# Twelve places for the experts' weights joined to six of 16 KB a partition

## The chip, the cores and the metric

The kernel runs on one core of a Trainium2 chip. What counts is the device time of one execution in microseconds (us); the time before is the median of three runs.

## The reference, cut to what matters

A sequence of 256 tokens of width 1024 goes through one transformer block of another kind (`first_block`) and then through two layers of the same kind. All arithmetic is in float32. A layer of the second part is a mixer (two attentions whose results are gated and merged) and a set of 16 experts, of which each chooses 32 tokens for itself.

```python
def hybrid_mixer(h, w_in, w_branch_a, w_branch_b, b_gate, sink_logit, w_out):
    proj = jnp.einsum('bsd,dc->bsc', h, w_in)
    qa, ka, va, qw, kw, vw, gates = jnp.split(proj, SPLITS, axis=-1)
    ...
    ya = jnp.einsum('bsc,cd->bsd', oa.reshape(B, S, DIL_OUT), w_branch_a)
    ...
    yb = jnp.einsum('bsc,cd->bsd', ob.reshape(B, S, WIN_Q), w_branch_b)
    g = jax.nn.sigmoid((gates + b_gate)...).reshape(B, S, N_BRANCH_2, D)
    merged = g[:, :, 0] * ya + g[:, :, 1] * yb
    return jnp.einsum('bsd,de->bse', merged, w_out)

def expert_choice_ffn(h, w_router, w_gate, w_up, w_down):
    cap = CAPACITY_FACTOR * S // N_EXPERTS          # 32 tokens
    aff = jax.nn.softmax(jnp.einsum('bsd,de->bse', h, w_router)..., axis=-1)
    gate, idx = lax.top_k(jnp.swapaxes(aff, 1, 2), cap)
    xe = h[bidx, idx]
    a = jnp.einsum('becd,edf->becf', xe, w_gate)
    u = jnp.einsum('becd,edf->becf', xe, w_up)
    ye = jnp.einsum('becf,efd->becd', jax.nn.silu(a) * u, w_down)
    return jnp.zeros_like(h).at[bidx, idx].add(gate[..., None] * ye)
```

Each expert has three weights of 1024 x 1024 float32 (4 MB each), so the experts of one layer read 192 MB and multiply each weight with 32 tokens only.

## The kernel before, in words

**Dense products.** Every dense weight comes in loads of one megabyte (`load`, L118: 128 partitions of 2048 floats) into a ring of three tiles named `w`. `split_w` makes of each half of such a tile (`hf` 0 and 1) a rounded high part on ScalarE (L124) and the remaining low part on VectorE (L125), in tiles `ws`; `mm3` (L130 to L132) then multiplies three times: high by high, high by low, low by high. A ring tile is free for its next load when both its halves are split. SP issues all of these loads, in the order of the program, and an issue that has to wait holds up those behind it.

**Mixer.** The loads of `w_in2` are numbered 0 to 22 by their second index. After the attentions, `gate(j)` takes the loads 15 + 2j and 16 + 2j, multiplies, and applies a tanh on ScalarE (L927). Between the gates lie the products of the branches: `w_br2` gives five loads, each tile's halves serve eight blocks of 128 columns (`blk`), and after ten blocks `merge` joins two results: VectorE adds them, ScalarE writes the high part of `M` (L270) and VectorE its low part. The order of the text is the order of the engines' queues: `gate(0)`, `gate(1)`, branch products for i = 0 and 1, `gate(2)`, two more, `gate(3)`, and the rest. So ScalarE's queue holds, in one row, the splits of loads 18 to 20, the cast of the attention's result `Y` (L157), the tanh of the gates and the copies for `M`.

**Experts.** A layer's 192 MB are cut into 192 chunks of one megabyte, 128 rows of 8 KB (`CH` = 2048 floats). `grouped` (L1172) takes them in order with `take()` and runs 16 matmuls on each, with four experts side by side on the array. `Experts.load` issues a chunk (L1045) into the next place of a fixed cycle of 21: `q`, four `a0`, six `a1`, `Ha`, `Hb`, `b`, three ring tiles `r`, four split tiles `s`; the first round has two more, `x`. In the profile the places' tiles are named `we`, and the two of `x` `W` and `XB`. The chunks of a layer's end (its last 16) skip `Ha` and `Hb` and are issued one behind the other, and the last chunk comes in two halves (128 x 1024).

```python
self.cycle = ["q"] + ["a0"] * NA0 + ["a1"] * NA + ["Ha", "Hb"] + ["b"] * NB + ["r"] * RING + ["s"] * NSPLIT
self.places = self.cycle + ["x", "x"]
...
src = a["w_exp"][self.l, i]
...
def pace(self):
    if len(self.have) < 1 + NA0 + NA:
        self.load(True)
```

**Chunks ahead of their layer.** While the mixer runs, the first places are filled: `prefetch(1, True)` in the query part, `pace()` behind each load of the gates and branches, and `prefetch(2, True)` at i = 5. A load that is paced this way first gets a copy of one column on GpSimd (L1040) from the newest split tile, so that it can't start before that split has been made. When the mixer ends, the remaining places are asked for with `take()` and from then on each place as soon as its last reader has ended.

`act_pair()` gives the two tiles `Ha` and `Hb` for the high and low part of the normed input, which the places of the same names reuse while the experts run.

Of the kernel before, what the change touches and what calls it, by code (L numbers as in the profile page):

```python
# [18 lines left out]
P = 128  # L19
# [36 lines left out]
ENDS = ((0, 512), (512, 256), (768, 256))  # L56

SCRATCH = 2048


@with_exitstack
def tile_net(ctx: ExitStack, tc: tile.TileContext, a, out):
# [98 lines left out]
    def act_pair():  # L161
        return tuple(hp.tile([P, KT, T], F32R, name=f"H{c}", tag=f"H{c}") for c in "ab")
# [531 lines left out]
    def mixer(l, h, stats, w0=None):  # L694

        with ExitStack() as es:
# [17 lines left out]
            xl.r2a.append(late.enter_context(tc.tile_pool(name=f"e{l}a0", bufs=NA0, side="right", reuse_waits="tile")))  # L714
# [83 lines left out]
            for i in range(4):  # L798
                parts_q(qws[i], load(w1[l, 2 + i]))
                xl.prefetch(1, True)  # L800
# [57 lines left out]
            xl.prefetch(1, True)  # L858
# [51 lines left out]
            xl.r2a.append(late.enter_context(tc.tile_pool(name=f"e{l}a", bufs=NA, side="right", reuse_waits="tile")))  # L910
# [21 lines left out]
            for i in range(8):  # L932
                if i % 2 == 0 and i < 6:
                    gate(i // 2 + 1)
                if i == 5:

                    xl.prefetch(2, True)
                ps = psd()
                for k in range(10):
                    if blk % 16 == 0:  # L940
                        w = load(a["w_br2"][l, blk // 16])
                        xl.pace()
                    if blk % 8 == 0:
                        wh, wl = split_w(sp, w, blk // 8 % 2)
                    b = blk % 8 * P
                    mm3(ps[:, 0:T] if k < 2 else ps[:, T:], cols(wh, b, P), cols(wl, b, P),
                        Y[:, 0, k, :], Y[:, 1, k, :], k in (0, 2), k in (1, 9))
                    blk += 1
                merge(M, i, [tgs[i // 2][:, b, i % 2, :] for b in range(2)], [ps[:, 0:T], ps[:, T:]])
# [58 lines left out]
    class Experts:  # L1008


        def __init__(self, l):
            self.l, self.r2a, self.r2b, self.at, self.dma = l, [], None, 0, None
            self.have, self.n = [], 0

            self.cycle = ["q"] + ["a0"] * NA0 + ["a1"] * NA + ["Ha", "Hb"] + ["b"] * NB + ["r"] * RING + ["s"] * NSPLIT
            self.places = self.cycle + ["x", "x"]

        def load(self, paced=False):
            i = len(self.have)
            end = i >= NCHUNK - sum(cn for _, cn in ENDS) * KT // 512  # L1020
            while True:
                where = self.places.pop(0)
                if not self.places:
                    self.places = list(self.cycle)

                if not (end and where in ("Ha", "Hb")):
                    break
            if where == "x":
                t = self.extra.pop(0).rearrange("p a d -> p (a d)")
            elif where == "s":  # L1030
                t = sp.tile([P, 2, 1024], F32, name="we", tag="ws").rearrange("p a d -> p (a d)")
            else:
                pool, tag = {
                    "q": (qp, "Qb"), "a0": (self.r2a[0], "w2"), "a1": (self.r2a[-1], "w2"), "b": (self.r2b, "w3"),
                    "r": (ring, "w"), "Ha": (hp, "Ha"), "Hb": (hp, "Hb"),
                }[where]
                t = pool.tile([P, CH], F32, name="we", tag=tag)
# [3 lines left out]
            src = a["w_exp"][self.l, i]  # L1041

            for c0, cn in ((0, 1024), (1024, 1024)) if i == NCHUNK - 1 else ((0, CH),):
                with tc.issue_after(self.dma.ins) if end else nullcontext():
                    self.dma = nc.sync.dma_start(t[:, c0 : c0 + cn], src[:, c0 : c0 + cn])  # L1045
            self.have.append(t)
# [5 lines left out]
        def pace(self):  # L1052

            if len(self.have) < 1 + NA0 + NA:
# [8 lines left out]
    def experts(l, last, xl, bp, xg, lg, rt):  # L1063
        nonlocal x
        with ExitStack() as es:
# [165 lines left out]
            for g in range(4):  # L1231
# [27 lines left out]
                else:  # L1259
                    if not last:  # L1260
                        h = act_pair()
                    for i, (c0, cn) in enumerate(ENDS):
                        if not last and c0 + cn == D:
                            xl.prefetch(NCHUNK - len(xl.have))
# [49 lines left out]
def _experts(*ws):  # L1314
# [11 lines left out]
    return np.concatenate(chunks, 0)  # L1326
# [139 lines left out]
```

## Time and profile before

| what | value |
|---|---|
| median of three runs | 1898.48 us (1895.02 to 1900.64) |
| the profiled execution | 1898.55 us, span 1896.8 us |
| mean granted clock of TensorE in it | 0.888 of full speed |
| TensorE busy | 1600.4 us, 84% of the span |
| VectorE / ScalarE / GpSimd busy | 823.2 / 629.2 / 46.3 us |
| moved by DMA | 562.49 MB, mean 297 GB/s |

The span runs from the first to the last instruction that the profiler recorded on the core; the device time of the same execution is 1.75 us longer. Busy shares are means over stretches of different kinds. In the slices of the page the first block ends near 500 us, the mixers take some 500 to 750 us and 1160 to 1430 us, and between and behind them lie the experts, where the rate of the transfers is highest and VectorE and ScalarE have next to nothing to do.

### The profile page before, as it was taken

The numbers are of one execution on the slowest core, as the hardware profiler recorded it, in microseconds if no ns is written. First come the engines' busy times: TensorE is split into PE (matmuls) and PEld (weight loads), VectorE is DVE, ScalarE is ACT, GpSimd is POOL, SyncE is SP. The second block draws the span as 40 slices with busy tenths as digits, with TensorE's granted clock in tenths as the row PEclk, the third lists the DMA queues.
The fourth block names the chain that finished last, engine by engine and source line by source line (L and its number), as shares of the span: only waits on it lengthen the run. The fifth ranks groups of instructions, "written<-read, shape, count | busy, mean of one in ns | idle before, by whom it ended". The sixth has DMA issues, their size and how long they took to land.

```text
span 1896.8 us, 27588 instructions
## 1 busy us (share of the span) xinstructions
PE 1600.4 (84%) x11434; PEld 1081.8 (57%) x11434; DVE 823.2 (43%) x1481; ACT 629.2 (33%) x1130; POOL 46.3 (2%) x72
## 2 busy tenths in 40 slices
PE   8999999999999988876767666999898866766665
PEld 7899999999998987220111102888896311101101
DVE  7688787996687556100000001687464100000001
ACT  5567646666566443100000001566443100000001
POOL 0100000000011000000000000010000000000000
PEclk9999999999999999887777768999999887867768
DMA  6454554554553367999999999832577999999998
GB/s 248 167 190 167 178 178 179 187 190 178 217 223 112 147 267 275 397 419 420 420 420 419 420 420 418 332 129 102 222 266 277 418 420 419 419 420 419 420 421 321
DMA packets 83829, 562.49 MB, mean 297 GB/s; under 512 B 9452, under 2 KB 14456, under 8 KB 16888
## 3 DMA queue, kind: packets, MB, share of 16 engines
q1 hardware_dynamic: 83544, 560.20, 74.7%
q8 instruction: 90, 1.47, 0.3%
q10 hardware_dynamic: 160, 0.52, 0.1%
q14 instruction: 35, 0.29, 0.0%
HBM read 558.84 MB, written 1.85 MB: 296 GB/s over the span
## 4 chain that ended last, share of the span: by engine, by line
PE 54%; DMA 43%; DVE 2%; ACT 1%; issue 0%; SPq 0%; ACTq 0%; DVEq 0%
DMA we<-in_w_exp_dram 42%; PE ps_d L130 14%; PE ps_d L131 14%; PE ps_d L132 14%; PE ps_t L257 1%; PE ps_g L1172 1%; PE ps_v L846 1%; DMA w<-in_w_in_dram 1%; PE ps_u L1172 1%; PE ps_s L772 1%; PE ps_s L878 1%; PE ps_s L773 0%; PE ps_s L374 0%; PE ps_t L1187 0%; PE ps_v L896 0%
## 5 line engine op out<-in xcount | busy, mean ns | idle before, releaser
L130 PE MATMUL ps_d<-Ha,ws 128*128 128x256 f32 x1408 | 404.9, 288 | 14.7 <-ACT Ha L177 7.9
L132 PE MATMUL ps_d<-Ha,ws 128*128 128x256 f32 x1408 | 404.9, 288 | 5.0 <-DVE ws L125 4.9
L131 PE MATMUL ps_d<-Hb,ws 128*128 128x256 f32 x1408 | 403.6, 287 | 0.7 <-DVE Hb L178 0.7
L125 DVE TENSOR_TENSOR ws<-w,ws 128x1024 fp32r<-128x1024 f32 x282 | 342.6, 1221 | 119.7 <-ACT ws L124 117.0
L124 ACT CAST ws<-w 128x1024 fp32r<-128x1024 f32 x282 | 293.3, 1047 | 256.0 <-PE ps_d L132 223.3
L130 PEld LDWEIGHTS ps_d<-Ha,ws 128*128 128x128 f32 x1408 | 273.0, 194 | 18.4 <-ACT Ha L177 7.9
L132 PEld LDWEIGHTS ps_d<-Ha,ws 128*128 128x128 f32 x1408 | 273.0, 194 | 8.3 <-DVE ws L125 6.1
L131 PEld LDWEIGHTS ps_d<-Hb,ws 128*128 128x128 f32 x1408 | 272.9, 194 | 3.5 <-issue 1.2
L1172 PE MATMUL ps_u<-we,W 128*32 128x512 f32 x992 | 187.8, 836 | 90.4 <-DMA we<-in_w_exp_dram 90.3
L1172 PE MATMUL ps_g<-we,W 128*32 128x512 f32 x1024 | 175.9, 789 | 71.9 <-DMA we<-in_w_exp_dram 71.8
L1172 PE MATMUL ps_e<-we,W 128*32 128x512 f32 (+1 forms) x1152 | 162.6, 669 | 64.2 <-DMA we<-in_w_exp_dram 64.1
L1172 PEld LDWEIGHTS ps_u<-we,W 128*32 128x32 f32 x992 | 25.4, 125 | 239.2 <-DMA we<-in_w_exp_dram 223.1
L1172 PEld LDWEIGHTS ps_g<-we,W 128*32 128x32 f32 x1024 | 26.5, 123 | 205.7 <-DMA we<-in_w_exp_dram 165.3
L1246 ACT ACTIVATE W<-ps_g 128x512 f32<-128x512 f32 x16 | 9.6, 597 | 381.4 <-PE ps_g L1172 381.4
L1172 PEld LDWEIGHTS ps_e<-we,W 128*32 128x32 f32 x1152 | 29.4, 120 | 163.6 <-DMA we<-in_w_exp_dram 121.1
L1248 DVE SCALAR_TENSOR_TENSOR W<-W,ps_u 128x512 f32<-128x512 f32 x16 | 11.0, 688 | 247.1 <-PE ps_u L1172 247.1
L1201 DVE COPY W<-ps_e 128x512 f32<-128x512 f32 (+1 forms) x18 | 11.4, 632 | 221.5 <-PE ps_e L1172 221.5
L1247 DVE SCALAR_TENSOR_TENSOR W<-W,ps_g 128x512 f32<-128x512 f32 x16 | 11.0, 688 | 208.1 <-ACT W L1246 208.1
L1253 ACT COPY W<-ps_t 128x512 f32<-128x512 f32 x16 | 9.4, 586 | 275.9 <-PE ps_t L1252 275.9
L130 PE MATMUL ps_d<-Y,ws 128*128 128x256 f32 x288 | 81.4, 283 | 0.0
L132 PE MATMUL ps_d<-Y,ws 128*128 128x256 f32 x288 | 81.4, 283 | 0.0
L131 PE MATMUL ps_d<-Y,ws 128*128 128x256 f32 x288 | 81.4, 282 | 0.0
(327 smaller groups left out, 2371.9 us busy)
## 6 DMA issues: line engine op xcount, KB each, us to landing
we<-in_w_exp_dram SPq DMA_DIRECT2D x378, 1024.0 KB, 19.9
w<-in_w_in_dram SPq DMA_DIRECT2D x46, 1024.0 KB, 4.9
w<-in_w_up_dram SPq DMA_DIRECT2D x22, 1024.0 KB, 4.8
w<-in_w_br_dram SPq DMA_DIRECT2D x18, 1024.0 KB, 4.9
w<-in_w_gate_dram SPq DMA_DIRECT2D x12, 1024.0 KB, 4.9
w<-in_w_out_dram SPq DMA_DIRECT2D x12, 1024.0 KB, 4.9
w<-in_w_down_dram SPq DMA_DIRECT2D x11, 1024.0 KB, 4.9
w<-in_w_rnn_dram SPq DMA_DIRECT2D x8, 1024.0 KB, 4.8
```

The costliest lines, as they stand in the source:

```text
L124: nc.scalar.copy(ws[:, 0], s)
L125: nc.vector.tensor_tensor(ws[:, 1], s, ws[:, 0].bitcast(F32), op=ALU.subtract)
L130: nc.tensor.matmul(ps, wh, xh, start=first, stop=False)
L131: nc.tensor.matmul(ps, wh, xl, start=False, stop=False)
L132: nc.tensor.matmul(ps, wl, xh, start=False, stop=last)
L257: nc.tensor.transpose(ps[:, i * P : i * P + P], b, ident)
L772: nc.tensor.matmul(ps, q, kh, start=True, stop=False)
L846: nc.tensor.matmul(po[64 * c : 64 * c + 64, :T], vw[:, k, kvh * 64 : kvh * 64 + 64], pts[c][:, k * T : k * T + T], start=k == 0, stop=k == 1,)
L878: nc.tensor.matmul(ps[:, o], qa[b, i, tk], ka[b, i, kr], start=True, stop=True)
L1172: nc.tensor.matmul(b[32 * e : 32 * e + 32, :cn], lhs[:, k, 32 * e : 32 * e + 32], cols(w, ((k - k0) * 4 + e) * cn, cn), start=k == 0, stop ...
L1201: nc.vector.tensor_copy(ye[:, s], E[:, :cn])
L1247: nc.vector.scalar_tensor_tensor(th, th, 1.0, G[n], op0=ALU.add, op1=ALU.mult)
```

## The change

Three kinds of places are joined in pairs: the four `a0` become two, the six `a1` three, and `Ha` and `Hb` one place `H`, each now 16 KB in every partition. A joined place is filled by one load of two megabytes, in 128 rows of 16 KB, and holds two chunks that follow each other; the host lays these two out as such rows. A list made ahead (`_plan`) says for each load its first chunk, the number of chunks and its place, and the host and the kernel both follow it. All other places keep one chunk of 128 rows of 8 KB, as do the last four chunks of a layer; a joined `H` that would reach into the last 16 is skipped. The cycle of places and the total room in SBUF stay the same. The chunks ahead of their layer are asked for in fewer and larger pieces: `prefetch` is called at three places of the query part's loop and not at two others, `pace()` does something on every second call only, and `prefetch(2, True)` becomes `prefetch(1, True)`. The two tiles of `act_pair()` are now halves of one.

```diff
+def _plan():
+    cycle = [("q", 1)] + [("a0", 2)] * (NA0 // 2) + [("a1", 2)] * (NA // 2) + [("H", 2)] + [("b", 1)] * NB
+    cycle += [("r", 1)] * RING + [("s", 1)] * NSPLIT
+    places, plan, i = cycle + [("x", 1)] * 2, [], 0
+    while i < NCHUNK:
+        where, n = places.pop(0)
+        places = places or list(cycle)
+
+        if where == "H" and i + n > NCHUNK - LAST:
+            continue
+        n = n if i < NCHUNK - 4 else 1
+        plan.append((i, n, where))
+        i += n
+    return plan
...
     def act_pair():
-        return tuple(hp.tile([P, KT, T], F32R, name=f"H{c}", tag=f"H{c}") for c in "ab")
+        H = hp.tile([P, 2, KT, T], F32R, name="H", tag="H")
+        return H[:, 0], H[:, 1]
...
             for i in range(4):
                 parts_q(qws[i], load(w1[l, 2 + i]))
-                xl.prefetch(1, True)
+                if i != 2:
+                    xl.prefetch(1, True)
...
             parts_q(qa0, load(w1[l, 6]))
-            xl.prefetch(1, True)
...
                 if i == 5:
 
-                    xl.prefetch(2, True)
+                    xl.prefetch(1, True)
...
         def load(self, paced=False):
...
+            i, m, where = self.plan.pop(0)
+            end = i >= NCHUNK - LAST
...
-                t = pool.tile([P, CH], F32, name="we", tag=tag)
+                size = 2 * CH if where in ("a0", "a1", "H") else CH
+                t = pool.tile([P, size], F32, name="we", tag=tag)
...
-            src = a["w_exp"][self.l, i]
...
+            src = a["w_exp"][self.l, i * P * CH : (i + m) * P * CH].rearrange("(p c) -> p c", p=P)
...
-            self.have.append(t)
+            self.have += [t[:, CH * j : CH * j + CH] for j in range(m)]
...
-            if len(self.have) < 1 + NA0 + NA:
+            self.asked += 1
+            if self.asked % 2 and len(self.have) < 1 + NA0 + NA:
                 self.load(True)
...
-    return np.concatenate(chunks, 0)
+    chunks = np.concatenate(chunks, 0)
+    return np.concatenate([chunks[i : i + n].transpose(1, 0, 2).reshape(-1) for i, n, _ in _plan()])
```

**SP's queue in the gates.** The first row is the first branch load of the first layer (`w_br2` 0), the second the next one; `w_7839` is load 19 of `w_in2`, `w_7899` load 20. Before:

```order
L118 DMA w_7743<-in_w_br2_dram 128x2048
L118 DMA w_7810<-in_w_br2_dram 128x2048
L1045 DMA we_7546<-in_w_exp_dram 128x2048
L1045 DMA we_7609<-in_w_exp_dram 128x2048
L1045 DMA we_7673<-in_w_exp_dram 128x2048
L118 DMA w_7839<-in_w_in2_dram 128x2048
L1045 DMA we_7736<-in_w_exp_dram 128x2048
L1045 DMA we_7745<-in_w_exp_dram 128x2048
L118 DMA w_7899<-in_w_in2_dram 128x2048
L1045 DMA we_7812<-in_w_exp_dram 128x2048
L118 DMA w_8006<-in_w_br2_dram 128x2048
```

and with the change, where `w_7821` is load 19 and `w_7881` load 20:

```order
L137 DMA w_7728<-in_w_br2_dram 128x2048
L137 DMA w_7795<-in_w_br2_dram 128x2048
L137 DMA w_7821<-in_w_in2_dram 128x2048
L1056 DMA we_7537<-in_w_exp_dram 128x4096
L1056 DMA we_7661<-in_w_exp_dram 128x4096
L1056 DMA we_7730<-in_w_exp_dram 128x4096
L137 DMA w_7881<-in_w_in2_dram 128x2048
L137 DMA w_7988<-in_w_br2_dram 128x2048
```

Load 19 stands right behind the second branch load now, and three joined loads of the experts stand between it and load 20, where three single ones stood ahead of load 19 and two between.

**ScalarE's queue at the same place.** L124 are the splits' high parts; `w_7680` is load 18, `w_7743` and `w_7810` the branch loads, `w_7839` load 19. Before:

```order
L124 CAST ws_7682<-w_7680 128x1024
L258 COPY pd_7423<-ps_t_7462 128x512
L157 CAST Y_5875<-ps_v_7468 128x256
L124 CAST ws_7709<-w_7680 128x1024
L124 CAST ws_7748<-w_7743 128x1024
L124 CAST ws_7775<-w_7743 128x1024
L927 ACTIVATE tg_7615<-tg_7615,hb_5873 128x256 x2
L124 CAST ws_7815<-w_7810 128x1024
L927 ACTIVATE tg_7615<-tg_7615,hb_5873 128x256 x2
L270 ACTIVATE M_7487<-m0_7784 128x256
L124 CAST ws_7841<-w_7839 128x1024
L124 CAST ws_7868<-w_7839 128x1024
```

With the change L143 are the splits; `w_7668` is load 18, `w_7728` and `w_7795` the branch loads, `w_7821` load 19. The rows begin with the second half of load 18:

```order
L143 CAST ws_7697<-w_7668 128x1024
L278 COPY pd_7414<-ps_t_7453 128x512
L176 CAST Y_5872<-ps_v_7459 128x256
L143 CAST ws_7733<-w_7728 128x1024
L143 CAST ws_7760<-w_7728 128x1024
L947 ACTIVATE tg_7603<-tg_7603,hb_5870 128x256 x2
L143 CAST ws_7797<-w_7795 128x1024
L143 CAST ws_7823<-w_7821 128x1024
L947 ACTIVATE tg_7603<-tg_7603,hb_5870 128x256 x2
L143 CAST ws_7850<-w_7821 128x1024
L290 ACTIVATE M_7478<-m0_7769 128x256
```

The second half of load 18 has moved ahead of the cast of `Y` (L157 before, L176 now); the first half of load 19 has moved to right behind the branch half, and both its halves stand ahead of the copies for `M` (L270 before, L290 now).

**SP's queue in the first layer's experts.** The names `W` and `XB` are the two places `x` at the end of the first round. Before:

```order
L1045 DMA W<-in_w_exp_dram 128x2048
L1045 DMA XB<-in_w_exp_dram 128x2048
L1045 DMA we<-in_w_exp_dram 128x2048 x168
L1045 DMA we<-in_w_exp_dram 128x1024 x2
L719 DMA sinks<-in_rows_dram 128x32
```

and with the change, where 128x4096 is a joined load:

```order
L1056 DMA W<-in_w_exp_dram 128x2048
L1056 DMA XB<-in_w_exp_dram 128x2048
L1056 DMA we<-in_w_exp_dram 128x2048 x2
L1056 DMA we<-in_w_exp_dram 128x4096
L1056 DMA we<-in_w_exp_dram 128x2048 x2
L1056 DMA we<-in_w_exp_dram 128x4096 x2
L1056 DMA we<-in_w_exp_dram 128x2048 x2
L1056 DMA we<-in_w_exp_dram 128x4096 x3
L1056 DMA we<-in_w_exp_dram 128x2048 x4
L1056 DMA we<-in_w_exp_dram 128x4096 x6
L1056 DMA we<-in_w_exp_dram 128x2048 x9
L1056 DMA we<-in_w_exp_dram 128x4096 x6
```

The row of single loads behind `XB` has become an alternation of joined and single ones; its later rounds are six joined and nine single loads each, and the layer ends with ten single loads and the two halves.

## Rows read from the trace of the kernel before

**Rows 1.** The page's span and its queues: packets, MB, share of 16 engines.

```profile
span 1896.8 us, 27588 instructions
...
q1 hardware_dynamic: 83544, 560.20, 74.7%
q8 instruction: 90, 1.47, 0.3%
```

**Rows 2.** Stretches: length, busy PE PEld DVE ACT POOL, PEclk, DMA share, GB/s.

```profile
650.00:745.00 95.00, 90.14 (x722) 86.44 (x722) 56.04 (x89) 40.90 (x59) 3.98 (x7) 0.98 0.73 279
783.00:1144.00 361.00, 253.35 (x1386) 54.47 (x1378) 24.69 (x39) 14.30 (x31) 0.00 (x0) 0.74 1.01 420
1466.00:1868.00 402.00, 279.26 (x1575) 58.86 (x1571) 27.62 (x44) 16.34 (x35) 0.00 (x0) 0.77 1.01 420
```

**Rows 3.** The chain that ended last, by line, in shares of the span.

```profile
DMA we<-in_w_exp_dram 42%; PE ps_d L130 14%; PE ps_d L131 14%; PE ps_d L132 14%; PE ps_t L257 1%; PE ps_g L1172 1%; PE ps_v L846 1%; DMA w<-in_w_in_dram 1%; PE ps_u L1172 1%; PE ps_s L772 1%; PE ps_s L878 1%; PE ps_s L773 0%; PE ps_s L374 0%; PE ps_t L1187 0%; PE ps_v L896 0%
```

**Rows 4.** DMA issues (KB, us to landing); SP's waits (us, times, longest).

```profile
we<-in_w_exp_dram SPq DMA_DIRECT2D x378, 1024.0 KB, 19.9
...
SPq L1045 <- DMA we<-in_w_exp_dram: 667.1, 316, 3.6
```

**Rows 5.** The chain in the second expert stretch: start us, us, what.

```profile
1483.54 19.90 DMA we<-in_w_exp_dram
...
1503.50 18.66 DMA we<-in_w_exp_dram
...
1522.23 19.89 DMA we<-in_w_exp_dram
```

**Rows 6.** The load queue from 147.5 to 149.5 us: packets, MB, share.

```profile
q1 hardware_dynamic: 143, 0.13, 20.9%
```

**Rows 7.** The load queue from 510 to 512 us.

```profile
q1 hardware_dynamic: 118, 0.88, 104.6%
```

**Rows 8.** ScalarE's timeline, 643 to 648.2 us: start, us, instruction, idle before.

```profile
646.44 1.05 ACT L124 CAST ws<-w 128x1024 fp32r<-128x1024 f32 x1 [0.91 <-PE ps_d L132]
```

**Rows 9.** ScalarE's timeline from 652 to 680 us.

```profile
652.62 0.37 ACT L157 CAST Y<-ps_v 128x256 fp32r<-128x256 f32 x1 [4.64 <-PE ps_v L902]
652.89 2.95 ACT L124 CAST ws<-w 128x1024 fp32r<-128x1024 f32 x3
...
664.42 0.42 ACT L270 ACTIVATE M<-m 128x256 fp32r<-128x256 f32 x1 [2.91 <-DVE m L269]
664.75 1.98 ACT L124 CAST ws<-w 128x1024 fp32r<-128x1024 f32 x2
...
675.64 0.91 ACT L927 ACTIVATE tg<-tg,hb 128x256 f32<-128x256 f32 x2 [7.27 <-DVE tg L213]
676.45 2.93 ACT L124 CAST ws<-w 128x1024 fp32r<-128x1024 f32 x3
```

**Rows 10.** SP's timeline from 640 to 662 us.

```profile
642.78 0.33 SPq L118 DMA_DIRECT2D w<-in_w_br_dram  x1
643.16 11.00 SPq L1045 DMA_DIRECT2D we<-in_w_exp_dram  x3
655.74 0.33 SPq L118 DMA_DIRECT2D w<-in_w_in_dram  x1
...
658.48 0.39 SPq L118 DMA_DIRECT2D w<-in_w_in_dram  x1
```

**Rows 11.** TensorE's waits, 650 to 745 us: us, times, longest.

```profile
PE ps_d L130 <- ACT ws L124: 2.7, 1, 2.7
PE ps_d L132 <- DVE ws L125: 2.2, 1, 2.2
```

**Rows 12.** Stretches behind the waits, columns as in rows 2.

```profile
679.00:683.00 4.00, 4.00 (x23) 4.00 (x23) 3.14 (x3) 1.43 (x2) 0.00 (x0) 0.57 0.53 150
1366.00:1369.00 3.00, 3.00 (x17) 3.00 (x17) 0.59 (x2) 0.00 (x0) 0.00 (x0) 0.58 0.99 396
1375.00:1379.00 4.00, 3.94 (x20) 3.94 (x21) 3.50 (x3) 2.66 (x4) 0.00 (x0) 0.57 0.17 23
```

**Rows 13.** The chain where the experts begin: start us, us, what.

```profile
763.91 1.85 PE ps_g L1172 x16
```

More of the change, by code (lines that the diff above doesn't have):

```diff
@@ L56 @@
 ENDS = ((0, 512), (512, 256), (768, 256))
+LAST = sum(cn for _, cn in ENDS) * KT // 512
 SCRATCH = 2048
+def _plan():
[11 more added lines that the diff above has]
+    return plan
 @with_exitstack
@@ L713, in mixer @@
             xl = Experts(l)
-            xl.r2a.append(late.enter_context(tc.tile_pool(name=f"e{l}a0", bufs=NA0, side="right", reuse_waits="tile")))
+            xl.r2a.append(late.enter_context(tc.tile_pool(name=f"e{l}a0", bufs=NA0 // 2, side="right", reuse_waits="tile")))
             att = es.enter_context(ExitStack())
@@ L909, in mixer @@
             att.close()
-            xl.r2a.append(late.enter_context(tc.tile_pool(name=f"e{l}a", bufs=NA, side="right", reuse_waits="tile")))
+            xl.r2a.append(late.enter_context(tc.tile_pool(name=f"e{l}a", bufs=NA // 2, side="right", reuse_waits="tile")))
             M = qp.tile([P, 2, KT, T], F32R, name="M", tag="Qa")
@@ L1012, in __init__ @@
             self.l, self.r2a, self.r2b, self.at, self.dma = l, [], None, 0, None
-            self.have, self.n = [], 0
-            self.cycle = ["q"] + ["a0"] * NA0 + ["a1"] * NA + ["Ha", "Hb"] + ["b"] * NB + ["r"] * RING + ["s"] * NSPLIT
-            self.places = self.cycle + ["x", "x"]
+            self.have, self.n, self.plan, self.asked = [], 0, _plan(), 0
         def load(self, paced=False):
[L1019 to L1027, printed above, removed]
+            i, m, where = self.plan.pop(0)
+            end = i >= NCHUNK - LAST
             if where == "x":
@@ L1034, in load @@
                     "q": (qp, "Qb"), "a0": (self.r2a[0], "w2"), "a1": (self.r2a[-1], "w2"), "b": (self.r2b, "w3"),
-                    "r": (ring, "w"), "Ha": (hp, "Ha"), "Hb": (hp, "Hb"),
+                    "r": (ring, "w"), "H": (hp, "H"),
                 }[where]
-                t = pool.tile([P, CH], F32, name="we", tag=tag)
+                size = 2 * CH if where in ("a0", "a1", "H") else CH
+                t = pool.tile([P, size], F32, name="we", tag=tag)
             if paced:
                 nc.gpsimd.tensor_copy(t[:, 0:1], turn[0][:, 0:1].bitcast(F32))
-            src = a["w_exp"][self.l, i]
-            for c0, cn in ((0, 1024), (1024, 1024)) if i == NCHUNK - 1 else ((0, CH),):
+            src = a["w_exp"][self.l, i * P * CH : (i + m) * P * CH].rearrange("(p c) -> p c", p=P)
+            for c0, cn in ((0, 1024), (1024, 1024)) if i == NCHUNK - 1 else ((0, m * CH),):
                 with tc.issue_after(self.dma.ins) if end else nullcontext():
                     self.dma = nc.sync.dma_start(t[:, c0 : c0 + cn], src[:, c0 : c0 + cn])
-            self.have.append(t)
+            self.have += [t[:, CH * j : CH * j + CH] for j in range(m)]
         def prefetch(self, n, paced=False):
@@ L1263, in experts @@
                         if not last and c0 + cn == D:
-                            xl.prefetch(NCHUNK - len(xl.have))
+                            xl.prefetch(len(xl.plan))
                             with tc.issue_after(xl.dma.ins):
```

## The prediction

> **What bounds the kernel now.** I read the page first: the span, and how busy the load queue is [rows 1]. Then the chain of waits, by line: transfers of the experts' weights hold 42% of the span and the three lines of the split dense products about as much together [rows 3]. So the kernel has two kinds of stretch, and a table by stage separates them [rows 2]. In the two expert stretches (783 to 1144 us and 1466 to 1868 us) the DMA engines are full, at 420 GB/s in both, and TensorE, at 253 of 361 us and 279 of 402 us, has room: there only the time of the transfers counts. In the mixers (650 to 745 us is the end of the first one) TensorE is busy for 90.1 of 95 us and the DMA engines for 73%: there only what makes TensorE stand counts. Last I looked at how the loads queue. A one-megabyte load takes 19.9 us from issue to landing, and SP waits 316 times for the landing of an earlier load [rows 4]. Eight loads stand in the queue at once, so a fixed cost that one load has before or after its data is hidden behind the seven others. What is left to save is what the engines themselves spend beside the bytes.
>
> **Joined loads in the expert stretches.** Of 192 chunks of a layer, 106 now come in 53 loads of two. Six of the 53 go out in the mixer; 47 a layer, 94 in all, lie in the full stretches (the order rows with 128x4096 behind XB count 47). The trace has no 16 KB row, so I bound what a joined load saves.
>
> Nothing, if the cost is by the byte alone or if the rows are cut again to 8 KB: 0.
>
> Low end above that: in the second layer one load of half a megabyte (the final gain, 128 rows of 4 KB) stands among the full ones. Pieces of the chain, each as long as eight loads, begin at 1483.54, 1503.50 and 1522.23 us [rows 5]: 19.96 us with eight full loads, 18.73 us with seven and the small one. A full load is 19.96 / 8 = 2.495 us, the small one 18.73 - 7 x 2.495 = 1.27 us. Both have eight packets on each engine; twice the small one less the full one is the part that doesn't go by bytes: 2 x 1.27 - 2.495 = 0.045 us. Joining two loads saves this once.
>
> High end: 128 packets of 1 KB, almost alone in 2 us, take 20.9% of 16 engines, or 6.69 us: 52 ns each [rows 6]. The 108 packets of 8 KB in another 2 us take 104.6%, 33.5 us: 310 ns each [rows 7] (the handful of 4-byte packets beside them counted as nothing). The slope is 258 ns for 7168 bytes, so 8 KB cost 295 ns and 15 ns are fixed. A joined load has eight packets on an engine where two loads have sixteen: 8 x 15 = 0.12 us.
>
> I take 0.075 us, nearer the half-megabyte load, since that stood in the full queue: 94 x 0.075 = 7.05 us. The ends give 0, 4.2 and 11.3 us.
>
> The Trainium skill's "DMA: Bandwidth & Descriptors", section "Why small descriptors are slow (HBM only)", gives each packet some three cycles beside its 32-byte beats, and each transfer 32 bytes of descriptors. With the 850 MHz that the page gives for the fabric that is an estimate of 4.7 ns a packet, 0.038 us a joined load, 3.5 us in all; the sum below would be 3.5 us higher by it. The trace's half-megabyte load comes close to it, its small packets lie at three times as much.
>
> **What the joined loads move in the mixer.** Here the order decides. The gates' loads 18, 19 and 20 share a ring of three with those of the branch weights, and each waits until its slot's halves are split. Before, ScalarE splits the first half of load 18 at 646.44 us [rows 8], then stands behind the cast of Y until 652.62 us, and splits the second at 652.89 us [rows 9]; load 19 goes out at 655.74 us and load 20 at 658.48 us [rows 10]. Load 19 is split only at 664.75 us, since ScalarE's merge of M stands ahead of it and waits for VectorE until 664.42 us [rows 9]. TensorE waits for that split for 2.2 us, and once more for load 20, 2.7 us [rows 11]; the second layer's answer has the same two rows.
>
> After, the second half of load 18 stands ahead of the cast of Y, where 646.44 us was its first half's time, so load 19 can go out when VectorE has its low part, some 2.4 us later: about 649 us instead of 655.74 us, to land some 5 us later. Its first half stands right behind the branch half ahead of it, and both its halves stand ahead of both merges. They are split before TensorE has ended the branch products ahead of them. The wait of 2.2 us goes, in both layers: -4.4 us. Work that hides the split: the branch products that TensorE still has.
>
> What is late next is load 20, for now all three joined loads (six megabytes, where five stood before, two of them already moving) go ahead of it. From 649 us: 4.8 us for load 19 on an idle queue, 6 x 2.495 = 15.0 us for the three, 2.5 us for load 20: 671.3 us, and up to 1.6 us for the last engine, 672.9 us. It was split at 676.45 us, behind the tanh of load 19's gates [rows 9], and is wanted 2.2 us sooner now: 674.25 us. So there is cover of 1 to 3 us, and the 2.7 us wait stays as it is, since it is the chain from load 19's last product over VectorE and ScalarE to the split.
>
> The three paced loads in the query part (five before, of one megabyte) are less tight: no instruction of ScalarE waits for a transfer there; I put that at nothing. POOL loses its copies for them, which nobody waits for now.
>
> The granted clock is an open term. After these waits it stood for some 3 us at its lower level, 1.2 GHz: means of 0.57 and 0.58 [rows 12]. Whether a fall comes with the one wait that stays I can't tell; with two waits there was one fall in the first layer and there were two in the second. I leave it out of the sum and put 1.5 us a layer into the range.
>
> **The start of an expert stretch.** The second round of places is asked for in the order chunk 23, 37, then the pair 24 and 25, where 24 alone stood second. The pair waits for two chunks to be used up. TensorE uses two in 1.85 us [rows 13], so the pair comes about a chunk, 0.9 us, later, part of which chunk 37 covers: +0.5 us a layer, +1.0 us (0 to 2). Later on TensorE is ahead of the loads and a place is free long before it is asked for. The tail of a layer stays: the last eleven chunks are single as before, and the last one still comes in two halves.
>
> **Sum.** The profiled execution took 1898.55 us (1.75 us around its span), within 0.1 us of the median 1898.48 us. 1898.55 - 7.05 - 4.4 + 1.0 = 1888.1 us; with the ends of the load's price alone 1895.2, 1890.9 and 1883.8 us.
>
> **Rivals.** *The transfers gain nothing* (rows cut to 8 KB, or cost by the byte): 1898.55 - 4.4 + 1.0 = 1895.2 us. For it: each MB of the full stretches takes the same 2.495 us, near what the bytes alone explain (8 x 295 ns = 2.36 us). Against it: the half-megabyte load and the small packets both show a fixed part. The Trainium skill's "DMA: Bandwidth & Descriptors", section "Rules for kernel authors", asks for 128 partitions and a megabyte or more in a transfer for full bandwidth, which the old loads meet; no run here shows where the gain of larger ones ends.
>
> *The new wait takes the place of the old.* If load 19 still goes out at 655.74 us, the three joined loads queue behind it, and load 20 lands at 655.74 + 4.8 + 15.0 + 2.5 = 678.0 us, 1.6 us after its split began before. TensorE stands for one long wait: +1.6 us in place of -2.2 us in the first layer, about nothing in the second, whose split came later by the clock's fall. 1898.55 - 7.05 + 1.0 + 1.6 = 1894.1 us. Against it stands the order of ScalarE's row.
>
> *Slower: a 16 KB packet costs more than two of 8 KB.* On queue q8 90 packets of 16 KB take 0.3% of 16 x 1896.8 us, 91 us: 1.01 us each, against 2 x 0.31 us [rows 1]. But these share the engines with q1's packets, and the time of one holds waits for the other. The place is the full stretches, 94 loads; the other terms leave -3.4 us, so the kernel is slower from 3.4 / 94 = 0.036 us a joined load on, 0.7% of its 4.99 us, and by over 0.3% from 0.097 us on. At 3% the time is 1898.55 - 3.4 + 94 x 0.15 = 1909.2 us.
>
> **How the numbers follow.** 0.3%, 5.7 us, is about what a measurement of this kernel can tell from no change: faster is below 1892.8 us, slower above 1904.2 us. Forecast 0.65, with a range of its own from 1883 to 1892 us; no gain in the transfers 0.15, of which a little falls under 1892.8 us with a quieter clock; the new wait 0.14, some of it too; slower 0.06. Faster 0.65 + 0.02 = 0.67, same 0.27, slower 0.06. The range reaches from the high end of the packet price to the transfers that gain nothing: 1882.5 to 1896.5 us, with 0.07 below and some 0.1 above.
>
> **What would show it.** In the expert stretches of the new trace the rate must rise to 423 or 424 GB/s (21 MB in 52.4 - 6 x 0.075 = 51.9 us), with about half as many 8 KB packets and the rest of 16 KB; at 420 the first rival holds, below it the last. In the gates the wait of TensorE for the low part from VectorE, 2.2 us, must be gone in both layers and load 19 must go out some 6 us sooner; a wait of 4 us or more for load 20's split means the second rival. The forecast is wrong if the price of 0.075 us is off by more than a half, or if a fall of the clock costs more than it did.

## The result, and the profile after

The changed kernel takes 1888.09 us (median of four runs, 1887.44 to 1890.49) against 1898.9 us: a ratio of 0.9948, with an interval of 0.993 to 0.9966. The forecast was 1888.1 us. Timed once more beside three variants it took 1887.11 us against 1900.65 us, a ratio of 0.9922 (0.9908 to 0.9936).

The span and the load queue on the page, and the issues of the experts' loads (count, KB each, us to landing), answer to [rows 1, 4]:

```profile
span 1886.0 us, 27355 instructions
...
q1 hardware_dynamic: 68280, 560.19, 74.5%
...
we<-in_w_exp_dram SPq DMA_DIRECT2D x106, 2048.0 KB, 27.1
we<-in_w_exp_dram SPq DMA_DIRECT2D x166, 1024.0 KB, 24.7
```

The same bytes go in 15,264 fewer packets: each of the 106 joined loads spares 128 rows and 16 packets of 4 bytes (144 x 106). By stage, with the columns and stretches of [rows 2]:

```profile
650.00:745.00 95.00, 92.34 (x742) 88.68 (x741) 55.95 (x90) 40.51 (x60) 0.56 (x3) 0.98 0.75 293
783.00:1144.00 361.00, 223.45 (x1390) 57.98 (x1382) 24.90 (x40) 13.83 (x31) 0.00 (x0) 0.83 1.01 424
1466.00:1868.00 402.00, 264.61 (x1586) 63.56 (x1578) 31.37 (x51) 19.38 (x43) 0.00 (x0) 0.79 1.01 423
```

The DMA engines are as full as before (1.01) and move 424 and 423 GB/s where it was 420: they spend less time beside the bytes. In the mixer TensorE is busy for 2.2 us more of the 95 us. Its waits from 640 to 745 us, where [rows 11] had two, are now one:

```profile
PE ps_d L149 <- ACT ws L143: 2.7, 1, 2.7
```

The second layer's gates give this row as well. SP's timeline from 636 to 690 us (start, us, instruction), beside [rows 10]:

```profile
644.46 0.33 SPq L137 DMA_DIRECT2D w<-in_w_br_dram  x1
650.45 0.33 SPq L137 DMA_DIRECT2D w<-in_w_in_dram  x1
650.83 4.73 SPq L1056 DMA_DIRECT2D we<-in_w_exp_dram  x3
658.55 0.33 SPq L137 DMA_DIRECT2D w<-in_w_in_dram  x1
```

Load 19 goes out at 650.45 us, where it was 655.74 us, then the three joined loads, then load 20 at 658.55 us, as before. ScalarE's timeline from 640 to 685 us, beside [rows 8, 9]:

```profile
648.12 1.05 ACT L143 CAST ws<-w 128x1024 fp32r<-128x1024 f32 x1 [0.91 <-PE ps_d L151]
...
654.30 0.37 ACT L176 CAST Y<-ps_v 128x256 fp32r<-128x256 f32 x1 [4.64 <-PE ps_v L922]
654.57 2.10 ACT L143 CAST ws<-w 128x1024 fp32r<-128x1024 f32 x2
...
664.21 1.05 ACT L143 CAST ws<-w 128x1024 fp32r<-128x1024 f32 x1 [0.89 <-PE ps_d L151]
667.12 0.42 ACT L290 ACTIVATE M<-m 128x256 fp32r<-128x256 f32 x1 [1.86 <-DVE m L289]
...
674.88 0.91 ACT L947 ACTIVATE tg<-tg,hb 128x256 f32<-128x256 f32 x2 [4.83 <-DVE tg L233]
675.69 2.92 ACT L143 CAST ws<-w 128x1024 fp32r<-128x1024 f32 x3
```

The second half of load 18 is split at 648.12 us, ahead of the cast of `Y`, and the last split of load 19 at 664.21 us, ahead of the copy for `M`. That copy still waits for VectorE, but no split stands behind it. The split of load 20 still stands behind the tanh at 674.88 us.

**Where the time went.** The trace has the same 11,434 matmuls of TensorE in every kernel of this study. Their order differs at a few hundred places inside the experts and is the same at the ends of the stages, so the starts of equal matmuls give the length of a stage. The numbers are us, worked out from the records of one profile each: gates from matmul 5150 to 5980 and from 8900 to 9720 (to the first chunks of the experts), experts from 5980 to 7702 (the first product of the next mixer) and from 9720 to 11433; in brackets how much of a gates' stage had the lower clock, 1.2 GHz. The kernels of the last eight lines are those of the experiments below.

| kernel | gates 1 | experts 1 | gates 2 | experts 2 |
|---|---|---|---|---|
| before | 117.42 (13.7) | 420.10 | 115.24 (13.7) | 421.64 |
| before, again | 118.26 (13.7) | 420.10 | 115.38 (13.7) | 421.73 |
| changed | 114.75 (13.7) | 416.39 | 111.59 (10.2) | 418.32 |
| changed, again | 112.84 (6.8) | 416.50 | 110.05 (6.8) | 418.00 |
| rows8k_one_dma | 112.82 (6.8) | 420.11 | 111.64 (10.2) | 421.68 |
| rows8k_two_dmas | 112.89 (6.8) | 420.22 | 111.64 (10.2) | 423.82 |
| mixer_as_before | 118.72 (17.1) | 416.33 | 115.29 (13.7) | 418.24 |
| rows4k | 114.70 (13.7) | 431.28 | 111.66 (10.2) | 434.56 |
| quads | 114.60 (13.7) | 416.18 | 111.61 (10.2) | 418.28 |
| pace_even | 110.90 (10.2) | 416.11 | 106.94 (6.8) | 419.77 |
| late_quads | 109.36 (6.8) | 416.64 | 107.50 (6.8) | 417.08 |
| late_sixes | 109.40 (6.8) | 415.75 | 107.01 (6.8) | 416.96 |

Of the span's 10.8 us (1896.8 to 1886.0) the experts' stages give 3.71 + 3.32 = 7.0 us and the gates 2.67 + 3.65 = 6.3 us. Other places give 2.5 us back: 1.6 us at the start of the first mixer, by a fall of the clock (matmuls 4025 to 4150 take 19.40 us in place of 17.84 us; see below), 0.8 us behind the last matmul, whose cause I did not follow, and 0.1 us before the mixer.

### The profile page after: what moved, and what is told of

Same layout as the page of the kernel before. It is cut to its first block, busy times and chain, and to the rows that moved or that the text cites. A ratio compares the mean times of both kernels' runs of the same rounds, so it can differ in the third digit from the quotient of the medians.

```text
span 1886.0 us, 27355 instructions
## 1 busy us (share of the span) xinstructions
PE 1555.5 (82%) x11434; PEld 1090.0 (58%) x11434; DVE 824.2 (44%) x1481; ACT 629.2 (33%) x1130; POOL 36.1 (2%) x60
## 4 chain that ended last, share of the span: by engine, by line
PE 53%; DMA 44%; DVE 1%; ACT 1%; issue 0%; SPq 0%; POOL 0%; ACTq 0%
DMA we<-in_w_exp_dram 42%; PE ps_d L149 14%; PE ps_d L150 14%; PE ps_d L151 14%; PE ps_t L277 2%; DMA XB<-in_rows_dram 1%; PE ps_v L867 1%; PE ps_g L1184 1%; DMA w<-in_w_in_dram 1%; PE ps_s L792 1%; PE ps_s L898 1%; PE ps_u L1184 1%; PE ps_s L793 1%; PE ps_t L1199 0%; PE ps_s L394 0%; PE ps_v L916 0%
## 5 line engine op out<-in xcount | busy, mean ns | idle before, releaser
L149 PE MATMUL ps_d<-H,ws 128*128 128x256 f32 x1408 | 404.8, 288 | 14.4 <-ACT H L197 7.6
L151 PE MATMUL ps_d<-H,ws 128*128 128x256 f32 x1408 | 404.4, 287 | 1.0 <-DVE ws L144 1.0
L150 PE MATMUL ps_d<-H,ws 128*128 128x256 f32 x1408 | 403.2, 286 | 0.2 <-DVE H L198 0.2
L143 ACT CAST ws<-w 128x1024 fp32r<-128x1024 f32 x282 | 293.8, 1046 | 263.9 <-PE ps_d L151 231.7
L149 PEld LDWEIGHTS ps_d<-H,ws 128*128 128x128 f32 x1408 | 273.0, 194 | 18.1 <-ACT ws L143 7.6
L151 PEld LDWEIGHTS ps_d<-H,ws 128*128 128x128 f32 x1408 | 272.7, 194 | 3.9 <-issue 1.7
L150 PEld LDWEIGHTS ps_d<-H,ws 128*128 128x128 f32 x1408 | 272.7, 194 | 2.9 <-issue 1.2
L1184 PE MATMUL ps_u<-we,W 128*32 128x512 f32 x992 | 171.4, 795 | 108.5 <-DMA we<-in_w_exp_dram 108.5
L1184 PE MATMUL ps_g<-we,W 128*32 128x512 f32 x1024 | 163.5, 749 | 81.8 <-DMA we<-in_w_exp_dram 81.8
L1184 PE MATMUL ps_e<-we,W 128*32 128x512 f32 (+1 forms) x1152 | 151.4, 649 | 69.9 <-DMA we<-in_w_exp_dram 69.9
L1184 PEld LDWEIGHTS ps_u<-we,W 128*32 128x32 f32 x992 | 29.9, 127 | 239.0 <-DMA we<-in_w_exp_dram 195.5
L1184 PEld LDWEIGHTS ps_g<-we,W 128*32 128x32 f32 x1024 | 30.5, 124 | 201.0 <-DMA we<-in_w_exp_dram 128.4
```

Source lines behind the costliest of these rows:

```text
L143: nc.scalar.copy(ws[:, 0], s)
L149: nc.tensor.matmul(ps, wh, xh, start=first, stop=False)
L150: nc.tensor.matmul(ps, wh, xl, start=False, stop=False)
L151: nc.tensor.matmul(ps, wl, xh, start=False, stop=last)
L1184: nc.tensor.matmul(b[32 * e : 32 * e + 32, :cn], lhs[:, k, 32 * e : 32 * e + 32], cols(w, ((k - k0) * 4 + e) * cn, cn), start=k == 0, stop ...
```

## The experiments

Theory A is the prediction's: half as many packets save some 0.08 us of the engines' time a joined load, and the new order of the queues ends one wait a layer. Against it stand B (fewer and larger transfers, or more bytes in the queue, are what counts), C (all of it is in the gates and the clock) and D (the gates gain from something other than the order).

**The changed kernel again**, as the mark for the next three.

> The changed kernel itself once more, as the mark beside the next three. Theory A (each joined load saves about 0.084 us of the DMA engines' time by having half as many packets, 94 times, and the gates lose a wait of 2.2 to 2.7 us a layer by a new order of the queues) and its rivals all expect 1888 us again, 10 to 11 us below the kernel before, and 423 to 424 GB/s in the two expert stretches.

Measured: 1887.11 us. The profiled one was the fastest of its six executions, 1881.49 us; its stages stand in the table as "changed, again".

**Rows of 8 KB in one transfer.** The host leaves the chunks as they were, and a joined load takes two blocks:

```diff
-    return np.concatenate([chunks[i : i + n].transpose(1, 0, 2).reshape(-1) for i, n, _ in _plan()])
+    return chunks.reshape(-1)
...
-            src = a["w_exp"][self.l, i * P * CH : (i + m) * P * CH].rearrange("(p c) -> p c", p=P)
+            src = a["w_exp"][self.l, i * P * CH : (i + m) * P * CH].rearrange("(m p c) -> p m c", p=P, m=m)
+            t3 = t.rearrange("p (m c) -> p m c", m=m)
...
-                    self.dma = nc.sync.dma_start(t[:, c0 : c0 + cn], src[:, c0 : c0 + cn])
+                    self.dma = nc.sync.dma_start(t3[:, :, c0 : c0 + cn], src[:, :, c0 : c0 + cn])
```

> The joined places, the order and the number of loads stay; each joined load is still one transfer of two megabytes, but its rows lie as two blocks of 128 rows of 8 KB, so it moves in twice as many packets. Theory A: the packets' saving goes, 94 x 0.084 = 7.9 us, so about 1896 us, 420 GB/s in the expert stretches, and the gates as in the changed kernel (no wait of 2.2 us for VectorE's low part). Rival B (fewer and larger transfers, or more bytes in the queue, are what counts): still 1888 us and 424 GB/s. Rival C (the whole gain lies in the gates and in the clock, and the rate is a by-product): 1888 us at 420 GB/s.

Measured: 1893.14 us, 6.0 us above the changed kernel on the same chip. What the load queue moved from 800 to 1140 us (packets, MB, share of 16 engines), first in the kernel before, then in the changed one, then here:

```profile
q1 hardware_dynamic: 19571, 142.53, 101.1%
```

```profile
q1 hardware_dynamic: 14062, 143.92, 100.7%
```

```profile
q1 hardware_dynamic: 18956, 142.61, 101.1%
```

A chunk has 1.0486 MB in this unit, so it takes 340 / (142.53 / 1.0486) = 2.501 us before, 2.477 us in the changed kernel and 2.500 us here. Loads of two megabytes in the same number and order keep 0.001 of the 0.024 us. The experts' stages, 420.11 and 421.68 us, are those of the kernel before. The packets of 4 bytes are as few as in the changed kernel (1548 and 1566 packets under 512 B in this stretch, 2173 before), so they do not make the gain either. B and C fall: the rows make the gain of the experts. The total lost 6.0 of the 7.9 us expected, the two stages 3.72 + 3.36 = 7.1 us. Whether the price belongs to the packet or to the length of the piece that it reads from memory, no run separates: a row is a packet in all of them.

**Rows of 8 KB in two transfers.** The same, with a `dma_start` for each half of a place, and a copy on GpSimd for each half of a paced one.

```diff
-            for c0, cn in ((0, 1024), (1024, 1024)) if i == NCHUNK - 1 else ((0, m * CH),):
+            for c0, cn in ((0, 1024), (1024, 1024)) if i == NCHUNK - 1 else [(CH * j, CH) for j in range(m)]:
```

> As the run before it, and each joined load is also issued as two transfers of one megabyte into the two halves of its place (a paced one gets the copy of one column for each half). The order of the gates stays that of the changed kernel. Theory A: the same 1896 us and 420 GB/s, since the packets are the same; the second issue costs SP time only and nobody waits for it. Rival B: if the number of transfers counts, 1896 us here and 1888 us in the run before it; if the bytes in the queue count, slower here than there.

Measured: 1895.4 us. Only the order of the gates and the tiles are left of the change, and that alone is worth a ratio of 0.9966 (0.9954 to 0.9978). Gates 1 has the length of the changed kernel at the same clock (112.89 and 112.84 us), with the one wait of 2.7 us. The second layer's experts take 2.1 us longer than with one transfer. By its own condition (slower here than there) rival B would claim them for the bytes in the queue, but a round of places takes 52.53 us here and 52.50 us there, so it is not the rate of the full stretch; where they go I did not follow.

**The mixer as before.** The loads ahead of a layer are single again, into halves of the joined places, and asked for where they were asked for before; joined loads begin with the second round.

```diff
+        if n == 2 and i < 12:
+            plan += [(i, 1, where + "+0"), (i + 1, 1, where + "+1")]
...
-                if i != 2:
-                    xl.prefetch(1, True)
+                xl.prefetch(1, True)
...
-            self.asked += 1
-            if self.asked % 2 and len(self.have) < 1 + NA0 + NA:
+            if len(self.have) < 1 + NA0 + NA:
```

> The loads ahead of a layer are single again, into the halves of the joined places, asked for at the places of the kernel before; SP's and ScalarE's queues in the gates read as before the change. From the second round of places on the loads are joined. Theory A: the two waits of the gates come back (2.2 and 2.7 us) and up to 1.1 us of lower clock in the second layer, so 1893 to 1894.5 us, with 423 to 424 GB/s in the expert stretches. Rival D (the gates' gain came from the joined tiles or from fewer copies on GpSimd, not from the order of the queues): 1888 to 1889 us.

Measured: 1894.63 us. TensorE's waits from 640 to 745 us:

```profile
PE ps_d L152 <- ACT ws L146: 2.7, 1, 2.7
PE ps_d L154 <- DVE ws L147: 2.2, 1, 2.2
```

Both waits of [rows 11] are back, in the second layer too, though the tiles are the joined ones; the experts keep their gain (416.33 and 418.24 us). So the tiles of D fall here. Its other half, the copies on GpSimd, falls with the run before: that one makes 26 of them, as this one and the kernel before do (the changed kernel 14), and has no wait of 2.2 us. The order of two queues came back at once, SP's and ScalarE's, and neither was put back alone. The 7.5 us against the changed kernel on the same chip are more than the two waits of 2.2 us. Beside the changed kernel's first profile (1887.84 us, near the median) the gates are 3.97 and 3.70 us longer: 2.2 us each is the wait, and the rest goes with 3.4 and 3.5 us more at the lower clock.

**The kernel before, a second profile.**

> The kernel before once more, for a second profile of it. Open is a fall of TensorE's granted clock at the start of the first mixer (510 to 515 us): it costs 1.1 to 2.0 us in the profiles of the changed kernel and of the three variants, and is absent from the one profile of the kernel before. If it is absent again, the change brings it; if it is there, it comes and goes with the execution. The expert stretches should show 2.501 us a megabyte again.

Measured: 1900.09 us in its one run. The stretch from 510 to 515 us, columns as in [rows 2], here and then in the changed kernel:

```profile
510.00:515.00 5.00, 5.00 (x30) 5.00 (x31) 3.42 (x8) 3.76 (x8) 0.18 (x1) 0.67 0.96 369
```

```profile
510.00:515.00 5.00, 4.86 (x28) 4.86 (x29) 3.44 (x9) 3.96 (x8) 0.32 (x2) 0.66 0.96 359
```

The fall is there without the change, and it is absent in three of the variants (rows4k, quads, pace_even). From matmul 4025 to 4150 both kernels take 19.40 us with it. It comes and goes, and its 1.6 us do not belong to the change.

**Rows of 4 KB**, the other way: the layout is cut into pieces of 1024 columns.

```diff
+    return np.concatenate([
+        chunks[i : i + n].reshape(n, P, 2, 1024).transpose(0, 2, 1, 3).reshape(-1) for i, n, _ in _plan()
+    ])
...
+            src = a["w_exp"][self.l, i * P * CH : (i + m) * P * CH].rearrange("(m p c) -> p m c", p=P, c=1024)
```

> The places, the loads and their order are those of the changed kernel, but every load of the experts lies in rows of 4 KB, so that a megabyte is 16 packets on each engine (8 in the kernel before). Theory A: the joined loads gave 0.084 us for eight packets less on each engine, 0.0105 us a packet, so a megabyte takes 2.501 + 8 x 0.0105 = 2.585 us; with 159 and 167 MB in the stretches behind the mixers, against 393 and 416 us now, that is 410 and 433 us and about 1922 us in all. Rival B (the number of transfers, or the bytes in the queue, decide): 1888 us. If the price of a packet grows as its rows get smaller, or the engines hide it, the time lies above or below 1922 us by what a packet costs.

Measured: 1915.07 us, a ratio of 1.0078 (1.0063 to 1.0094) to the kernel before. The load queue from 800 to 1140 us:

```profile
q1 hardware_dynamic: 35439, 138.91, 102.4%
```

That is 340 / (138.91 / 1.0486) = 2.567 us a chunk: eight more packets on each engine cost 0.066 us over the kernel before, 8 ns each, where I had put 10.5 ns. The direction is A's and the size three quarters of it; the total came 7 us under the expectation, of which the smaller price explains some 6 us (0.018 us for each of 326 chunks).

**Larger places.** Two places of 32 KB a partition, from the second round on:

```diff
-    cycle = [("q", 1)] + [("a0", 2)] * (NA0 // 2) + [("a1", 2)] * (NA // 2) + [("H", 2)] + [("b", 1)] * NB
+    cycle = [("q", 1)] + [("a0", 4), ("a4", 4), ("a1", 2), ("H", 2)] + [("b", 1)] * NB
...
+        if n == 4 and i < 12:
+            plan += [(i, 2, where + "+0"), (i + 2, 2, where + "+2")]
...
```

> The two a0 places become one of 32 KB a partition, two of the three a1 places another; from the second round on each is one load of four megabytes in rows of 32 KB (16 such loads a layer), while in the first round each is still filled by two joined loads at the same points. Theory A: each saves eight packets on each engine again, 0.084 us, 16 x 2 x 0.084 = 2.7 us: 1885 us where the changed kernel takes 1888 us, and about 424.5 GB/s. Rival E (rows above 16 KB save nothing, being cut again): 1888 us. Rival F (larger places come free later, and TensorE waits for four megabytes at once): above 1888 us, with pauses of the DMA engines in the stretches.

Measured: 1886.51 us, 0.9931 (0.9918 to 0.9943), which can't be told from the changed kernel. Theory A and rival F hold in part, and E falls. In the full stretches a round of 21 MB takes 51.85 us (from the ends of all its packets between 800 and 1140 us), 0.17 us less than the changed kernel's 52.02 us, or 0.083 us for each of the two loads. At the start it is lost again, as the stretches from 760 us on show, first of the quads, then of the changed kernel's second profile:

```profile
760.00:765.00 5.00, 5.00 (x50) 2.18 (x51) 0.00 (x0) 0.37 (x1) 0.00 (x0) 1.00 0.86 333
765.00:770.00 5.00, 5.00 (x48) 2.02 (x44) 0.00 (x0) 0.37 (x1) 0.00 (x0) 1.00 0.88 356
```

```profile
760.00:765.00 5.00, 5.00 (x51) 1.89 (x53) 0.00 (x0) 0.37 (x1) 0.00 (x0) 1.00 1.02 419
765.00:770.00 5.00, 5.00 (x48) 2.01 (x44) 0.00 (x0) 0.37 (x1) 0.00 (x0) 1.00 0.98 413
```

The first load of four megabytes waits until four chunks are used up (SP waits for TensorE for up to 4.2 us there), and the engines pause: (419 + 413 - 333 - 356) x 5 us = 0.7 MB late, 1.7 us.

**The other half of the pacing.** One word: the joined loads of the gates go out at the second, fourth and sixth asking.

```diff
-            if self.asked % 2 and len(self.have) < 1 + NA0 + NA:
+            if self.asked % 2 == 0 and len(self.have) < 1 + NA0 + NA:
```

> The changed kernel with one edit: the joined loads of the gates go out at every second asking counted from the second, not from the first. SP's queue then has two joined loads between load 19 and load 20 in place of three, and in ScalarE's queue the splits of load 20 stand right behind the copies for M and ahead of the tanh of load 19's gates. Theory A (these queues' order is what makes TensorE wait): the wait of 2.7 us that is left in each layer goes too, 5.4 us, with up to 1.5 us of lower clock behind each: 1880 to 1883 us. Rival G (load 20's transfer is what is late next, so the wait is for its landing): the wait stays or grows, 1888 us or more. The expert stretches stay at 2.477 us a megabyte.

Measured: 1877.83 us, 0.9885 (0.9871 to 0.9898), faster than both kernels and 2 us below the expected range: against the changed kernel's first profile the gates are 3.85 and 4.65 us shorter, with 3.5 and 3.4 us less at the lower clock, and the second layer's experts 1.45 us longer. TensorE has no wait for a split left from 645 to 700 us, nor in the second layer's gates. ScalarE's timeline from 663 to 678 us:

```profile
...
666.36 0.42 ACT L290 ACTIVATE M<-m 128x256 fp32r<-128x256 f32 x1 [1.86 <-DVE m L289]
668.88 0.42 ACT L290 ACTIVATE M<-m 128x256 fp32r<-128x256 f32 x1 [2.11 <-DVE m L289]
669.21 1.03 ACT L143 CAST ws<-w 128x1024 fp32r<-128x1024 f32 x1
670.58 1.05 ACT L143 CAST ws<-w 128x1024 fp32r<-128x1024 f32 x1 [0.34 <-PE ps_d L151]
...
674.41 0.91 ACT L947 ACTIVATE tg<-tg,hb 128x256 f32<-128x256 f32 x2
```

Load 20 goes out at 657.79 us with two joined loads ahead of it in place of three, lands at 668.16 us by the trace, and is split at 669.21 us, ahead of the tanh. Rival G falls. Two things moved at once, SP's queue and ScalarE's: in the changed kernel load 20 lands at 673.72 us, so a split moved ahead of the tanh alone would have had to wait for it. Which share each has was not tried alone.

**Both together, and larger still.** The even pacing, with places of 32 KB that take joined loads in the first two rounds (`i < 36`), and then with `a1` as one place of 48 KB.

> The kernel of the run with the even pacing, with the places of 32 KB, but in the first two rounds these are filled by joined loads of two megabytes, so that nothing waits for four chunks to be used up at the start of a stretch. Theory A: 14 loads of four megabytes a layer save 0.083 us each, 2.3 us in both layers, and the rate at the start of the stretch (333 and 356 GB/s between 760 and 770 us with the quads, 419 and 413 with the changed kernel) stays at that of the changed kernel: 1875.5 us, against 1877.8 us with the even pacing alone. Rival F (the large places themselves lose what their packets save): 1878 us.

Measured: 1876.93 us, 0.9878 (0.9857 to 0.9899). The rate at the start stays (397 and 415 GB/s from 760 to 770 us), and a round takes 51.85 us. The second layer's experts are 2.7 us shorter than with the even pacing alone, which had lost 1.45 us there, but the first layer's are 0.5 us longer, with 0.5 MB less landed when the stage begins; why, I did not find. The total can't be told from the run with even pacing.

> As the run before it, with all of a1 as one place of 48 KB a partition: a load of six megabytes where one of four and one of two stood, 7 a layer. Theory A: another 7 x 2 x 0.083 = 1.2 us: 1874.3 us. Rival F: up to 14 MB of the 21 are in the queue at once, places come free too late, the DMA engines pause or TensorE waits: 1876 us or more, with the pauses in the rows of the stretches.

Measured: 1874.6 us, 0.9864 (0.9849 to 0.988), the fastest. A round takes 51.76 us, 0.09 us less again, and no DMA slice of the full stretch falls below nine tenths. Against the even pacing the first layer's experts take 0.4 us less and the second layer's 2.8 us less. The part between them (matmuls 7702 to 8900) takes 156.91 us against 158.18 us; a fall of the clock of 3.4 us stayed away there. The intervals of the last three overlap: shown is the rate, not the order of the three totals.

## Why the prediction was right, point by point

**The joined load.** I took 0.075 us between 0.045 and 0.12 us. The round of 21 MB went from 52.53 to 52.02 us, with six joined loads: 0.024 us a chunk x 21 / 6 = 0.084 us a load, and 94 x 0.084 = 7.9 us where 7.05 us stood. 12% were missing. The measured price lies in the middle of the two ends, so leaning to the half-megabyte load was not borne out. That load was read too low: 18.73 - 7 x 2.495 is 1.265 us, which gives 0.035 us and not 0.045 us, and rows4k, with the same two row lengths all through the full stretch, gives 0.066 us. The high end was read too high: the packets' own times, from which it came, give 2 x 315 - 616 = 14 ns a packet in the new trace, where the rate gives 10.5 ns. The packets' times add up to 100.7 to 102.4% of the engines' span in these stretches, so some overlap, and their differences are more than what the engines lose. That two errors on either side left the choice near was luck. By the estimate from the Trainium skill's "DMA: Bandwidth & Descriptors", section "Why small descriptors are slow (HBM only)", it would have been 0.038 us and 3.5 us; here the measurement decides, at more than twice that.

**The start of a stretch.** 1.0 us for both layers was foreseen. (The piece of 16 matmuls in [rows 13] is two chunks, as the prediction took it: the trace has eight matmuls a chunk there, not the 16 named in the part on the experts.) The stages of the experts give 7.0 of the 7.9 us. Not all of the missing 0.9 us went to the start: rows8k_one_dma has the same places, sizes and order, and its two stages are only 0.01 and 0.04 us longer than before, though its rounds are 0.03 us shorter. I put the start at some 0.25 us a layer by that (eight rounds of 0.03 us, an estimate), half of what stood in the sum; the rest is open. The quads show the same mechanism at a larger size.

**The gates.** The wait of 2.2 us is gone in both layers, load 19 goes out 5.3 us sooner (6 us foreseen, and in this execution the work ahead of it came 1.7 us later), and mixer_as_before brings the wait back with the old queues. One cause was overlooked. The prediction put the late split of load 19 down to the copy for `M` that stood ahead of it until 664.75 us, but by the packets load 19 itself had landed only at some 664.4 us (its last 4-byte packet ended at 663.95 us, and its neighbours' landings stand 0.4 us behind theirs). Moving the split ahead of that copy alone would have saved 0.4 us at most; now load 19 lands at 655.29 us and is split from 661.45 us on. The change moved both, so the 2.2 us went as forecast. That the next one late is load 20 held too: it landed at 673.72 us (671.3 to 672.9 us worked out) and was split at 675.69 us, so there were 2 us of cover where I had 1 to 3 us. That the wait of 2.7 us which stays is the tanh's chain and not the transfer was right by the trace, and pace_even removed it. That the loads of the query part cost nothing held as well: from matmul 4025 to 5150 the profiles without the fall of the clock (before, rows4k, quads, pace_even) all take 149.96 us.

**The clock.** I left it out of the sum. In the second layer 3.5 us of the lower clock went with the wait, and gates 2 gained 3.65 us in place of 2.2 us; the three profiles with the old order of the gates have 13.7 us there and all the others 10.2 or 6.8 us. The fall at the start of the mixer, which I did not foresee at all, gave 1.6 us back. So the agreement to 0.1 us is partly chance: -7.0 and -6.3 us stand in place of -6.05 and -4.4 us, and 2.5 us elsewhere went the other way.

**The rivals.** The transfers' rate rose, so the first falls. No wait took the old one's place, and load 19 did not go out at its old time, so the second falls. A packet of 16 KB takes 616 ns in the full stretches by the trace's packet records (mean), less than two of 8 KB with 315 ns each, so the third falls. The 1.01 us of queue q8 was not the price of a row of 16 KB; that it holds waits for other packets no run shows.

## What to carry to other kernels

Where the DMA engines are full, look at the packets and not at the number of transfers: longer rows in a partition gained about 1% of the full stretches here, and two transfers put into one without longer rows 0.001 us a megabyte. Make places large only where nothing waits for them: a large place at the start of a stretch gave back in one pause what its packets saved over the whole. Where loads are paced into a stretch that another engine bounds, look at the order in which they leave the shared queue: here one word moved some 10 us, part of it by the clock.

## What the runs showed of the hardware that was not expected

Rows kept paying over a factor of twelve in length. A packet less on an engine saved 8 ns from rows of 4 KB to 8 KB (0.066 us / 8), 10.5 ns from 8 to 16 KB (0.084 / 8), 10.4 ns from 16 to 32 KB (0.083 / 8), and about 11 ns for the step to 48 KB (0.09 / 8).

TensorE's granted clock fell to 1.2 GHz in stages with equal instructions for 13.7 us in one profile of the changed kernel and for 6.8 us in the other; the stage was 1.9 us shorter in the second. The two executions' spans differ by 6.4 us (1886.0 and 1879.6), about the width of the interval of the result, so a single profile does not tell whether a fall belongs to a change.
